# State-space mixer: phases on GpSimd, states of every step summed on TensorE, a skip product of 128 rows

## The chip, the cores and the metric

The kernel runs on one core of one Trainium2 chip. The metric is the device time of one execution in microseconds (us), as a median of runs. In the profile the engines are PE (TensorE; PEld is its weight load), DVE (VectorE), ACT (ScalarE), POOL (GpSimd) and SP (SyncE, which here only issues DMAs).

## The reference

Two layers over 512 tokens of 1024 channels, all in float32. Layer 0 mixes the tokens with a state-space model (S5), layer 1 with causal latent attention; each is followed by a layer norm, a feed-forward part with squared relu, and another norm. The change lies in S5 alone:

```python
# 64 groups of 16 channels, 64 complex states per group
mag = exp(lr * dt);  a = mag * (cos(li * dt) + i sin(li * dt))
bb  = (a - 1) / lam * b
h_t = a * h_(t-1) + bb u_t                    # complex, over 512 tokens
y   = Re(c h) + d_skip * u                    # the skip is d_skip * u
y   = gelu(y)
val, gate = split(y @ w_glu);  mix = (val * sigmoid(gate)) @ w_out
```

## The kernel before

The core runs S5 first (about the first 150 us), then glu, projections, feed-forward and attention, in which TensorE works nearly without a pause. In S5 the 64 groups are cut into eight eighths (e = 0 to 7), one per step of a loop. The 512 tokens are 64 chunks of 8. Real and imaginary parts of 64 states lie on 128 partitions.

Ahead of the loop, `s5_tables` (L157) makes the tables of all groups on VectorE, the phase `f` of a chunk in turns among them, and `s5_powers` (L214) their powers. A step then takes these parts:

- `s5_phase(e)` (L269): r = k f less its nearest integer, for 64 chunks k and 8 groups. It is called twice. The first call makes eight ScalarE products (L275) and one ScalarE addition that rounds (L276); the second is one VectorE operation (L278).
- `s5_trig(e)`: the sine and cosine of r on ScalarE (L284, L287, L288).
- `s5_w`, `s5_q` (L264, L294, L364): outer products W and Q on VectorE.
- `s5_p`: eight transposes of W on TensorE (L304), copied out by ScalarE (L307); `s5_s`: the chunks' inputs (L315).
- `s5_rot`, `s5_add`, `s5_scan` (L323 to L343): rotate by the phase on VectorE, add the swapped half on TensorE (L330, L331), scan over the chunks on VectorE (L341), rotate back.
- `s5_turn` and `s5_state` (L346, L354): the states H = hc + x. In steps 0 and 1 (`S5_WHOLE`) TensorE adds hc too (L351) and ScalarE copies H out of PSUM (L356); in the other six steps TensorE makes x alone (L352) and VectorE adds hc (L359).
- `s5_t`: the response within a chunk, TT, on TensorE with 32 columns of weights (L378, L380), and onto its diagonal the skip d, by products with 32 rows (L384); ScalarE spreads TT (L387). `s5_y`: outputs (L396, L397), then a gelu (L404), a trip through DRAM and a split.

The order on each engine is the order in which the code issues, since S5 runs under a manual schedule. Step e makes the phase of step e + 2. TensorE fills waits with products that nothing reads (`warm`) in steps 0 and 1, and with parts of the glu (L573 to L575) later. Tiles that `self.f` makes come from a ring of ten, so that one may have to wait for the readers of the tile that held its place.

Of the kernel before, what the change touches and what calls it, by code (L numbers as in the profile page):

```python
# [76 lines left out]
class Net:  # L77
# [37 lines left out]
    def turns(self, out, x, tmp):  # L115
        """x less its nearest integer"""
        v = self.nc.vector
        yield v.tensor_scalar(tmp, x, MAGIC, MAGIC, op0=ALU.add, op1=ALU.subtract)
        yield v.tensor_tensor(out, x, tmp, op=ALU.subtract)

    def angle(self, k, out, x):
        """x to [-pi, pi], and its absolute value in k"""
        v = self.nc.vector
        yield v.tensor_scalar(k, x, 1.0 / TWO_PI, MAGIC, op0=ALU.mult, op1=ALU.add)
        yield v.tensor_scalar(k, k, MAGIC, None, op0=ALU.subtract)
        for i, part in enumerate(PI_PARTS):
            yield v.scalar_tensor_tensor(out, k, -part, x if i == 0 else out, op0=ALU.mult, op1=ALU.add)
        yield v.tensor_scalar(out, out, 3.1415925, -3.1415925, op0=ALU.min, op1=ALU.max)
        yield v.scalar_tensor_tensor(k, out, -1.0, out, op0=ALU.mult, op1=ALU.max)
# [27 lines left out]
    def s5_tables(self, pool):  # L157
# [25 lines left out]
        def phase():  # L183
            yield v.tensor_tensor(t1, li, dt, op=ALU.mult)
            yield from self.angle(t2, th, t1)
            nc.scalar.activation(t1, th, AF.Sin)
            nc.scalar.activation(t2, t2, AF.Sin, bias=self.col(3), scale=-1.0)
            # phase of a whole chunk of 8 tokens, in turns
            yield v.tensor_scalar(f, th, 8.0 / TWO_PI, None, op0=ALU.mult)
            yield from self.turns(f, f, t7)  # L190
# [11 lines left out]
        # coef = (a - 1) / lam  # L202
# [11 lines left out]
    def s5_powers(self, pool, i, j):  # L214
        """powers of a, and their products with coef, for eighths i to j"""
# [13 lines left out]
    def s5_static(self, pool):  # L229
        ms = self.nc.gpsimd.memset  # L230
        self.dd = pool.tile([32, 64, 16], F32, name="dd")
        self.nc.sync.dma_start(out=self.dd, in_=self.a["s5d"])
# [25 lines left out]
    def s5_outer(self, pool, e, dst, n, t_re, t_im, i, sign):  # L258
        """three operations, to be issued in turn"""
# [9 lines left out]
    def s5_phase(self, e):  # L269
        """the phase of k chunks, in turns"""  # L270
        st, f = self.st[e], self.tab["f"]
        if "r" not in st:
            st["r"], st["rt"] = self.f("r", [128, 8, 64]), self.f("rt", [128, 8, 64])
            for g in range(8):
                self.nc.scalar.mul(st["r"][:, g, :], self.c[:, C_KK:C_KK + 64], f[:, 8 * e + g:8 * e + g + 1])  # L275
            self.nc.scalar.activation(st["rt"], st["r"], AF.Identity, bias=self.col(8), scale=-1.0)  # L276
        else:
            self.nc.vector.scalar_tensor_tensor(st["r"], st["rt"], MAGIC, st["r"], op0=ALU.subtract, op1=ALU.add)  # L278
# [12 lines left out]
    def s5_w(self, pool, e):  # L291
        """W: response of the state to an input"""
# [5 lines left out]
    def s5_p(self, e):  # L298
        """P = (a W)^T of every group"""
# [10 lines left out]
    def s5_s(self, e):  # L310
        """inputs of the chunks"""
# [7 lines left out]
    # states before every chunk: a real recurrence in the rotating frame  # L319
# [26 lines left out]
    def s5_turn(self, e):  # L346
        self.st[e]["x"] = x = self.psum()
        hc, hs = self.st[e]["g"]
        whole = e in S5_WHOLE
        if whole:  # L350
            self.nc.tensor.matmul(x, self.ident, hc, start=True, stop=False)  # L351
        self.nc.tensor.matmul(x, self.c[:, C_NSW64:C_NSW64 + 128], hs, start=not whole, stop=True)  # L352

    def s5_state(self, e):  # L354
        if e in S5_WHOLE:
            self.nc.scalar.copy(self.H[:, :, 1:64], self.st[e]["x"].rearrange("p (g k) -> p g k", k=64)[:, :, 0:63])  # L356
            return
        hc, x = [z.rearrange("p (g k) -> p g k", k=64)[:, :, 0:63] for z in (self.st[e]["g"][0], self.st[e]["x"])]
        self.nc.vector.tensor_tensor(self.H[:, :, 1:64], hc, x, op=ALU.add)  # L359

    def s5_q(self, pool, e):
        """Q: response to the state before a chunk"""
# [6 lines left out]
    def s5_t(self, e):  # L369
        """TT: response within a chunk, with the skip on its diagonal"""  # L370
        act, pe = self.nc.scalar, self.nc.tensor
        W, TT, Q, one = self.W[e % 2], self.TT[e % 2], self.st[e]["Q"], self.c[0:32, C_E:C_E + 64]
# [16 lines left out]
    def s5_y(self, e):  # L389
        """outputs, in rows (position, channel)"""  # L390
# [9 lines left out]
    def s5_gelu(self, e):  # L400
        """their gelu, in rows (channel, group) by way of DRAM"""
# [12 lines left out]
    def warm(self, out, n, src=None):  # L414
        """products that nothing reads, while there is nothing else: the tensor engine's clock is halved after a pause"""
# [7 lines left out]
    def s5(self, pool, u0, early):  # L423
        """returns the split gelu'd outputs and the sums of the first units of the glu over them, but the last"""
# [13 lines left out]
        self.s5_phase(0)  # L438
# [8 lines left out]
        def partial(n):  # L447
            """some products of the glu that are ready"""
# [10 lines left out]
        for e in range(NT):  # L459
# [5 lines left out]
            if e == 0:  # L465
                self.s5_t(0)
                self.s5_phase(1)
# [35 lines left out]
            if e + 2 < NT:  # L503
                self.s5_phase(e + 2)
# [6 lines left out]
    def weights(self, units):  # L511
        """units: list of (dram AP, shape); loaded and split in this order"""
# [39 lines left out]
    # the second part of a split can be put off, for the vector engine not to wait  # L552
# [24 lines left out]
    def dense_steps(self, ps, w, col, act, tok=slice(0, T), n=None):  # L577
        """ps [128, tokens] = w[:, :, col].T @ act, over the k tiles of act; stops after every one"""
# [20 lines left out]
    def rstd(self, out, sq, n, eps_col):  # L599
        """sq: tiles [128, tokens] of squares, still to be summed over the partitions; n: their number; stops after the sums and before  # L600
        their spreading"""
# [13 lines left out]
        # the mean of s / var and 1 / s, for a root s that is nearly right  # L615
# [17 lines left out]
    class Norm:  # L633
        """z: 8 tiles [128, T] of the channels, normed in place, then split into act or stored to out"""
# [5 lines left out]
        def add(self, j):  # L640
            """z[j] is there"""
# [7 lines left out]
        def mean(self, last=None):  # L649
            """last: a tile that is not in the sum yet"""  # L650
# [10 lines left out]
        def squares(self, parts=(0,)):  # L661
            """z less its mean, and its squares, summed over the tiles from every one of parts to the next"""
# [22 lines left out]
        def finish(self):  # L685
            """stops after every tile"""
# [27 lines left out]
        def keep(self):  # L714
            """the normed z itself, for the next residual; stops after every tile"""
# [5 lines left out]
    def rms_norm(self, x, g, n):  # L721
        """x: tiles in PSUM [128, T]; the split normed tiles, with the tokens put in order; stops after every tile,
        after the sums, before and after their spreading"""
# [26 lines left out]
    # tokens of layer 0 stand in the order (position in a chunk, chunk)  # L750
# [10 lines left out]
    class Ahead:  # L761
        """the first three units of the next layer"""
# [15 lines left out]
    def feed_forward(self, u0, h, act, hid, g, b, follow=None, out=None, aside=iter(())):  # L778
        """hid: the hidden tiles of the first three units; aside: work for the vector engine that fits in"""
# [32 lines left out]
    def boundary(self, u, src, settle, z, g, b, follow=None, out=None, pool=None, begun=None):  # L812
        """the last four units before a layer norm, the norm, and the first three after it: half of the tokens is
        normed while the other is computed"""
# [29 lines left out]
        with self.tc.manual_schedule():  # L844
# [56 lines left out]
            def run2(i, tok, ms=(0, 1)):  # L901
                """both tiles of a unit in turn, for its rows may still be on their way"""
# [42 lines left out]
    def project(self, u0, act, h, g, b, follow, order=None, zpool=None, pool=None, begun=None):  # L945
        """layer norm of ALPHA * h + act @ w, for a [DM, DM] matrix in four units"""
# [32 lines left out]
    def rope(self, x, then):  # L979
        """x [128, T]: two heads of 64 rows; rotated in place"""  # L980
# [78 lines left out]
    def values(self, p, a):  # L1059
        """two of the four token tiles, for both heads"""  # L1060
# [12 lines left out]
    def query_rope(self, p):  # L1073
        """rotary parts of both heads, scaled"""
# [26 lines left out]
    def scores(self, hd, t):  # L1101
        """exponentials of the scores of query tile t [128 queries, keys up to them]"""
# [22 lines left out]
    def transposed(self, hd, t):  # L1125
        """into room for the two parts of p^T of one head: key tile k has the queries from 128 k on"""
# [15 lines left out]
    def attention(self, u0, latent, kvg, qg):  # L1142
# [10 lines left out]
        def fill(steps):  # L1153
            """products of the next layer's first unit with the heads that are there"""
# [11 lines left out]
        def ahead(p, s):  # L1166
            """what the coming queries need, some of it for the next two heads"""
# [50 lines left out]
# eighths whose gelus, and whose splits, are due in a step of S5: gelus in pairs, for fewer loads of tables  # L1218
S5_GELUS = [[0], [1], [], [2, 3], [], [4, 5], [6], [7]]
S5_SPLITS = [[], [0], [1], [], [2], [3], [4], [5, 6]]  # L1220
# steps in which a unit of weights is split; spare products of a step; steps whose states the tensor engine adds up
S5_UNITS = [1, 3, 6]
S5_WARM = [[2, 2, 2], [6, 3, 2]] + 6 * [[0, 0, 0]]
S5_WHOLE = [0, 1]
# [63 lines left out]
def host_s5(x, lam_re, lam_im, log_dt, b_re, b_im, c_re, c_im, d):  # L1288
    """layout only"""
# [16 lines left out]
def layout(x, positions, ln_mix_g, ln_mix_b, ln_ffn_g, ln_ffn_b, w_ff1, w_ff2, ssm_lam_re, ssm_lam_im, ssm_log_dt,  # L1306
# [10 lines left out]
    def cut(w, cols):  # L1317
        """[K, N] -> [units, 128, K / 128, cols]"""
# [40 lines left out]
```

## Time and profile before

| what | us |
|---|---|
| median of 3 runs (1204.53 to 1206.81) | 1206.55 |
| span of the profiled execution, first to last instruction | 1203.0 |
| TensorE busy | 1171.5 (97%) |
| VectorE busy | 693.1 (58%) |
| ScalarE busy | 510.2 (42%) |
| GpSimd busy | 2.6 (0%) |

The profiled execution is listed by its span alone; 3.55 us lie between that and the median. A busy time counts an engine's own instructions, and a matmul's end is modelled, so a full TensorE row says that there was no pause, not that each product was as short as it could be. The shares are of the whole span; S5 has its own, which the rows below give by stretches.

### The profile page before, as it was taken

What the parts mean: (1) busy time and instruction counts of PE and PEld (TensorE: products, weight loads), DVE (VectorE), ACT (ScalarE), POOL (GpSimd) and SP (SyncE); (2) the same over time, 40 slices, a digit from 0 to 9 for tenths busy, and PEclk for the clock granted to TensorE, in tenths of its full rate; (3) what the DMA queues carried; (4) which work ended last, traced back from release to release, by engine and by line L of the source; (5) the groups of instructions that cost most, each with busy time, mean ns of one, the idle gap of its engine ahead of it and who ended that gap; (6) DMA issues with size and microseconds to landing.
All of it is one profiled execution on the core that took longest, in us unless ns stands there. A gap on an engine that the chain in (4) does not pass through costs nothing.

```text
span 1203.0 us, 16076 instructions
## 1 busy us (share of the span) xinstructions
PE 1171.5 (97%) x6634; PEld 1002.4 (83%) x6634; DVE 693.1 (58%) x1244; ACT 510.2 (42%) x867; POOL 2.6 (0%) x12
## 2 busy tenths in 40 slices
PE   5899999999999999999999999999999999999996
PEld 3778888999888888888999788889988888888896
DVE  8999552487444434425585787768733442533456
ACT  4888551337314414213356566534731421322324
POOL 0000000000000000000000000000000000000000
PEclk9999999999999999999999999999999999999998
DMA  4122361214232222323311112221322222331212
GB/s 166 47 89 95 97 205 66 96 45 133 72 120 70 105 105 70 105 105 105 127 35 38 43 51 71 71 72 57 119 70 105 73 103 105 105 105 70 105 36 71
DMA packets 28905, 106.16 MB, mean 88 GB/s; under 512 B 10624, under 2 KB 12800, under 8 KB 18208
## 3 DMA queue, kind: packets, MB, share of 16 engines
q1 hardware_dynamic: 27680, 103.04, 25.1%
q10 hardware_dynamic: 1152, 2.10, 0.5%
q8 instruction: 52, 0.85, 0.3%
q14 instruction: 21, 0.17, 0.0%
HBM read 100.93 MB, written 4.19 MB: 87 GB/s over the span
## 4 chain that ended last, share of the span: by engine, by line
PE 91%; DVE 6%; ACT 2%; issue 1%; DMA 0%; ACTq 0%; DVEq 0%
PE ps L574 27%; PE ps L575 27%; PE ps L573 27%; PE ps L397 1%; PE ps L396 1%; PE ps L315 1%; PE ps L1110 1%; PE ps L380 1%; PE ps L1136 1%; PE ps L607 1%; PE ps L1111 1%; PE ps L352 1%; DVE tmpw L264 1%; PE ps L630 1%; PE ps L330 0%
## 5 line engine op out<-in xcount | busy, mean ns | idle before, releaser
L573 PE MATMUL ps<-hh,whi 128*128 128x512 f32 (+1 forms) x704 | 245.0, 348 | 0.0
L574 PE MATMUL ps<-hl,whi 128*128 128x512 f32 (+1 forms) x704 | 243.7, 346 | 0.0
L575 PE MATMUL ps<-hh,wlo 128*128 128x512 f32 (+1 forms) x704 | 243.6, 346 | 0.0
L530 ACT CAST whi<-raw 128x2048 fp32r<-128x2048 f32 (+1 forms) x91 | 165.9, 1834 | 162.7 <-DMA raw<-in_ff 141.6
L532 DVE TENSOR_TENSOR wlo<-raw,whi 128x1024 fp32r<-128x1024 f32 (+2 forms) x182 | 206.4, 1176 | 30.6 <-ACT whi L530 28.6
L573 PE MATMUL ps<-fh,whi 128*128 128x512 f32 (+1 forms) x608 | 216.8, 357 | 0.0
L574 PE MATMUL ps<-fl,whi 128*128 128x512 f32 (+1 forms) x608 | 216.1, 355 | 0.0
L575 PE MATMUL ps<-fh,wlo 128*128 128x512 f32 (+1 forms) x608 | 216.1, 355 | 0.0
L772 ACT ACTIVATE relu<-ps 128x512 f32<-128x512 f32 x64 | 38.1, 595 | 265.8 <-PE ps L575 265.8
L573 PEld LDWEIGHTS ps<-hh,whi 128*128 128x128 f32 x704 | 133.6, 190 | 16.4
L574 PEld LDWEIGHTS ps<-hl,whi 128*128 128x128 f32 x704 | 133.7, 190 | 16.2
L575 PEld LDWEIGHTS ps<-hh,wlo 128*128 128x128 f32 x704 | 133.7, 190 | 16.1
L774 DVE TENSOR_TENSOR relu<-relu 128x512 f32<-128x512 f32 x64 | 44.2, 690 | 169.2 <-ACT fh L773 169.2
L573 PEld LDWEIGHTS ps<-fh,whi 128*128 128x128 f32 x608 | 114.9, 189 | 16.5
L574 PEld LDWEIGHTS ps<-fl,whi 128*128 128x128 f32 x608 | 114.9, 189 | 16.3
L575 PEld LDWEIGHTS ps<-fh,wlo 128*128 128x128 f32 x608 | 114.9, 189 | 16.1
L790 DVE TENSOR_TENSOR z<-z,ps 128x512 f32<-128x512 f32 (+1 forms) x60 | 34.7, 579 | 119.8 <-PE ps L575 119.8
L573 PE MATMUL ps<-yh,whi 128*128 128x512 f32 x128 | 52.3, 410 | 0.0
L670 ACT ACTIVATE q<-z 128x256 f32<-128x256 f32 x64 | 25.0, 418 | 59.8 <-DVE z L668 59.8
L575 PE MATMUL ps<-yh,wlo 128*128 128x512 f32 x128 | 49.7, 390 | 0.0
L574 PE MATMUL ps<-yl,whi 128*128 128x512 f32 x128 | 49.7, 390 | 0.0
L775 DVE TENSOR_TENSOR fl<-relu,fh 128x512 fp32r<-128x512 f32 x64 | 44.2, 691 | 2.1
(255 smaller groups left out, 1744.3 us busy)
## 6 DMA issues: line engine op xcount, KB each, us to landing
raw<-in_ff SPq DMA_DIRECT2D x64, 1024.0 KB, 4.8
raw<-in_glu SPq DMA_DIRECT2D x8, 1024.0 KB, 5.1
raw<-in_w_out SPq DMA_DIRECT2D x4, 1024.0 KB, 5.0
raw<-in_wo SPq DMA_DIRECT2D x4, 1024.0 KB, 4.7
raw<-in_kvq SPq DMA_DIRECT2D x3, 1024.0 KB, 4.9
raw<-in_attq SPq DMA_DIRECT2D x4, 576.0 KB, 3.8
bc<-in_s5x SPq DMA_DIRECT2D x8, 256.0 KB, 4.6
u<-in_s5x SPq DMA_DIRECT2D x8, 256.0 KB, 5.1
```

Source lines behind the costliest of these rows:

```text
L264: v.tensor_tensor(o, self.tab[t][:, 0:n, G].rearrange("p m g -> p g m").unsqueeze(3).to_broadcast([128, 8, n, 16]), bc[:, j].unsqueeze(2). ...
L315: self.nc.tensor.matmul(s[:, g * 64:g * 64 + 64], st["P"][g // 4][:, 128 * (g % 4):128 * (g % 4) + 128], st["U"][:, g, :], start=True, sto ...
L530: self.nc.scalar.copy(hi, raw)
L532: self.put_off(lambda c=c: self.nc.vector.tensor_tensor(lo[:, c], raw[:, c], hi[:, c].bitcast(F32), op=ALU.subtract))
L573: pe.matmul(ps, whi, ahi, start=start, stop=False)
L574: pe.matmul(ps, whi, alo, start=False, stop=False)
L575: pe.matmul(ps, wlo, ahi, start=False, stop=stop)
L670: act.activation(qs[j], zj, AF.Square)
L772: self.nc.scalar.activation(r, ps, AF.Relu)
L774: self.nc.vector.tensor_tensor(r, r, r, op=ALU.mult)
L775: self.nc.vector.tensor_tensor(lo, r, hi.bitcast(F32), op=ALU.subtract)
L790: v.tensor_tensor(z[m][:, tok], z[m][:, tok], ps, op=ALU.add)
```

## The change

It has three parts, and comments and docstrings are gone throughout.

```diff
-        self.dd = pool.tile([32, 64, 16], F32, name="dd")
-        self.nc.sync.dma_start(out=self.dd, in_=self.a["s5d"])
+        self.dd = pool.tile([128, 64, 16], F32, name="dd")
+        for rows in (slice(32, 64), slice(64, 128)):
+            ms(self.dd[rows], 0.0)
+        self.nc.sync.dma_start(out=self.dd[0:32], in_=self.a["s5d"])
...
     def s5_phase(self, e):
-        st, f = self.st[e], self.tab["f"]
-        if "r" not in st:
-            st["r"], st["rt"] = self.f("r", [128, 8, 64]), self.f("rt", [128, 8, 64])
-            for g in range(8):
-                self.nc.scalar.mul(st["r"][:, g, :], self.c[:, C_KK:C_KK + 64], f[:, 8 * e + g:8 * e + g + 1])
-            self.nc.scalar.activation(st["rt"], st["r"], AF.Identity, bias=self.col(8), scale=-1.0)
-        else:
-            self.nc.vector.scalar_tensor_tensor(st["r"], st["rt"], MAGIC, st["r"], op0=ALU.subtract, op1=ALU.add)
+        st, p = self.st[e], self.nc.gpsimd
+        r, rt = st["r"], st["rt"] = self.f("r", [128, 8, 64]), self.f("rt", [128, 8, 64])
+        p.tensor_tensor(r, self.c[:, C_KK:C_KK + 64].unsqueeze(1).to_broadcast([128, 8, 64]),
+                        self.tab["f"][:, 8 * e:8 * e + 8].unsqueeze(2).to_broadcast([128, 8, 64]), op=ALU.mult)
+        p.tensor_scalar(rt, r, MAGIC, MAGIC, op0=ALU.add, op1=ALU.subtract)
+        p.tensor_tensor(r, r, rt, op=ALU.subtract)
...
     def s5_turn(self, e):
-        whole = e in S5_WHOLE
-        if whole:
-            self.nc.tensor.matmul(x, self.ident, hc, start=True, stop=False)
-        self.nc.tensor.matmul(x, self.c[:, C_NSW64:C_NSW64 + 128], hs, start=not whole, stop=True)
+        self.nc.tensor.matmul(x, self.ident, hc, start=True, stop=False)
+        self.nc.tensor.matmul(x, self.c[:, C_NSW64:C_NSW64 + 128], hs, start=False, stop=True)
...
     def s5_state(self, e):
-        if e in S5_WHOLE:
-            self.nc.scalar.copy(self.H[:, :, 1:64], self.st[e]["x"].rearrange("p (g k) -> p g k", k=64)[:, :, 0:63])
-            return
-        hc, x = [z.rearrange("p (g k) -> p g k", k=64)[:, :, 0:63] for z in (self.st[e]["g"][0], self.st[e]["x"])]
-        self.nc.vector.tensor_tensor(self.H[:, :, 1:64], hc, x, op=ALU.add)
+        self.nc.scalar.copy(self.H[:, :, 1:64], self.st[e]["x"].rearrange("p (g k) -> p g k", k=64)[:, :, 0:63])
...
-        W, TT, Q, one = self.W[e % 2], self.TT[e % 2], self.st[e]["Q"], self.c[0:32, C_E:C_E + 64]
+        W, TT, Q, one = self.W[e % 2], self.TT[e % 2], self.st[e]["Q"], self.c[:, C_E:C_E + 64]
```

The second calls of `s5_phase` are gone from `s5`, and so is `S5_WHOLE`. The 96 added rows of `dd` are zero.

On GpSimd (POOL) the program had, behind the memsets of the tables, nothing up to its end:

```order
L240 MEMSET H 128x8
L242 MEMSET TT_186 128x1024
L242 MEMSET TT_187 128x1024
L1354 UNCONDITIONAL_BRANCH
L1354 ISA [waits barrier_Pool_Activation_PE_DVE_SP_gather]
```

It now has, in the same place, three operations for each of the eight phases, of which the first three phases are (r_203 is the phase of step 0, r_240 of step 1, r_381 of step 2):

```order
L244 MEMSET TT_189 128x1024
L275 ISA
L275 TENSOR_TENSOR r_203<-c,f 128x512 [waits DMAHW1_49,DVE_49]
L277 TENSOR_SCALAR rt_204<-r_203 128x512 [waits Pool_49]
L278 TENSOR_TENSOR r_203<-r_203,rt_204 128x512 [waits Pool_49]
L275 TENSOR_TENSOR r_240<-c,f 128x512
L277 TENSOR_SCALAR rt_241<-r_240 128x512 [waits Pool_49]
L278 TENSOR_TENSOR r_240<-r_240,rt_241 128x512 [waits Pool_49]
L275 TENSOR_TENSOR r_381<-c,f 128x512 [waits Activation_49]
L277 TENSOR_SCALAR rt_382<-r_381 128x512 [waits Activation_49,Pool_49]
L278 TENSOR_TENSOR r_381<-r_381,rt_382 128x512 [waits Pool_49]
```

The first waits for the table `f` from VectorE; nothing holds the next six but what is named, so GpSimd takes them one behind the other.

On ScalarE (ACT), at the same place, before (behind the two sines of the tables):

```order
L275 ACTIVATE r_201<-c,f 128x64 [waits DVE_49]
L275 ACTIVATE r_201<-c,f 128x64 x7
L276 ACTIVATE rt_202<-r_201,c 128x512 [waits Activation_49]
L275 ACTIVATE r_244<-c,f 128x64 x8
L276 ACTIVATE rt_245<-r_244,c 128x512 [waits Activation_49]
L284 ACTIVATE rt_202<-r_201 128x512 [waits DVE_49]
L307 COPY P_268<-ps_263 128x512 [waits PE_49]
```

and now:

```order
L284 ACTIVATE rt_204<-r_203 128x512 [waits Pool_49]
L307 COPY P_257<-ps_252 128x512 [waits PE_49]
L307 COPY P_264<-ps_259 128x512 [waits PE_49]
L287 ACTIVATE si_250<-r_203,c 128x512
L288 ACTIVATE co_249<-rt_204,c 128x512 [waits Activation_49]
```

The products of the phase are out of this queue; L284 waits for GpSimd now, with the copies of P behind it. On VectorE the L278 rows are gone and the rows around them keep their order.

On TensorE (PE), in step 2 (ps_676 is x, ps_684 the inputs of step 3), before:

```order
L304 MATMUL ps_655<-c,W_190 128x128 x4
L304 MATMUL ps_662<-c,W_190 128x128 x4
L352 MATMUL ps_676<-hs_671,c 128x512
L315 MATMUL ps_684<-u_297,P_660 128x64 x4
L315 MATMUL ps_684<-u_297,P_667 128x64 x4
```

and now (ps_650 is x):

```order
L304 MATMUL ps_629<-c,W_192 128x128 x4
L304 MATMUL ps_636<-c,W_192 128x128 x4
L349 MATMUL ps_650<-hc_644,c 128x512
L350 MATMUL ps_650<-hs_645,c 128x512
L315 MATMUL ps_659<-u_286,P_634 128x64 x4
L315 MATMUL ps_659<-u_286,P_641 128x64 x4
```

One product more stands between the transposes and the inputs of the next step; the same holds in steps 3 to 7.

## Rows read from the trace of the kernel before

**Rows 1.** Engines by stretch (start:end, length, busy us, clock, DMA share, GB/s).
```profile
20.00:40.00 20.00, 18.18 (x135) 14.07 (x136) 19.86 (x37) 14.35 (x31) 0.00 (x0) 1.00 0.00 1
...
60.00:80.00 20.00, 19.45 (x149) 14.95 (x150) 18.87 (x20) 16.40 (x37) 0.00 (x0) 1.00 0.35 118
80.00:100.00 20.00, 19.53 (x151) 15.97 (x149) 19.63 (x22) 18.95 (x41) 0.00 (x0) 1.00 0.47 132
100.00:120.00 20.00, 20.00 (x174) 16.70 (x174) 18.45 (x21) 14.71 (x33) 0.00 (x0) 1.00 0.08 28
```
**Rows 2.** Chain that ended last, 0 to 280 us (start, length, engine, tile, line).
```profile
20.16 0.60 DVE r L278
...
24.26 0.68 DVE gc L323
...
31.99 0.60 DVE hs L343
...
48.57 0.64 PE ps L304 x4
...
105.00 1.06 PE ps L330 x2
...
110.56 0.86 PE ps L352 x2
...
119.67 1.06 PE ps L330 x2
```
**Rows 3.** Timeline, VectorE and GpSimd, 0 to 10 us (start, length; idle in brackets).
```profile
1.25 1.84 POOL L242 MEMSET TT<- 128x1024 f32 x2
...
2.80 0.34 DVE L133 TENSOR_SCALAR scr<-par 128x64 f32<-128x64 f32 x1 [2.80 <-DMA par<-in_s5p]
...
6.91 0.19 DVE L133 TENSOR_SCALAR scr<-scr 128x64 f32<-128x64 f32 x1
...
9.29 0.22 DVE L119 TENSOR_TENSOR f<-f,scr 128x64 f32<-128x64 f32 x1
```
**Rows 4.** GpSimd memsets by line (ns minimum/median/maximum).
```profile
L238 POOL MEMSET W<- x2: 205/206/207, 0.9 to 1.0; 128x128 f32 x2
...
L242 POOL MEMSET TT<- x2: 953/953/953, 1.3 to 2.1; 128x1024 f32 x2
```
**Rows 5.** Timeline, ScalarE, 14 to 50 us.
```profile
20.79 0.63 ACT L284 ACTIVATE rt<-r 128x512 f32<-128x512 f32 x1 [5.82 <-DVE r L278]
...
22.27 0.73 ACT L287 ACTIVATE si<-r,c 128x512 f32<-128x512 f32 x1
...
47.39 0.72 ACT L287 ACTIVATE si<-r,c 128x512 f32<-128x512 f32 x1
```
**Rows 6.** Timeline, TensorE, step 4: the skip's products and their neighbours.
```profile
117.44 0.21 PE L378 MATMUL ps<-Q,W 128*32 128x16 f32 x2
117.50 0.36 PE L380 MATMUL ps<-Q,W 128*32 128x112 f32 x2
117.79 0.41 PE L384 MATMUL ps<-dd,c 32*32 32x64 f32 x4
118.13 0.23 PE L378 MATMUL ps<-Q,W 128*32 128x16 f32 x2
118.21 0.36 PE L380 MATMUL ps<-Q,W 128*32 128x112 f32 x2
118.41 0.21 PE L378 MATMUL ps<-Q,W 128*32 128x16 f32 x2
```
**Rows 7.** Waits, 16 to 150 us (waiter, releaser, us in total, times, longest).
```profile
PEld ps L384 <- issue: 2.8, 16, 0.2
```
**Rows 8.** Timeline, TensorE, steps 2 and 3: pauses in brackets.
```profile
66.51 1.10 PE L352 MATMUL ps<-hs,c 128*128 128x512 f32 x2 [0.55 <-ACT si L287]
...
80.75 1.10 PE L352 MATMUL ps<-hs,c 128*128 128x512 f32 x2 [0.47 <-DVE hs L343]
```
**Rows 9.** ScalarE products that go, by line (ns minimum/median/maximum).
```profile
L275 ACT ACTIVATE r<-c,f x64: 331/337/363, 9.5 to 113.8; 128x64 f32<-128x64 f32 x64
```

More of the change, by code (lines that the diff above doesn't have):

```diff
@@ L437, in s5 @@
         self.s5_w(pool, 0)
-        self.s5_phase(0)
         self.s5_trig(0, self.s5_p)
@@ L466, in s5 @@
                 self.s5_t(0)
-                self.s5_phase(1)
             partial(2 * early)
@@ L502, in s5 @@
                 self.s5_powers(pool, 2, NT)
-            if e + 2 < NT:
-                self.s5_phase(e + 2)
         partial(len(todo))
@@ L1223 @@
 S5_WARM = [[2, 2, 2], [6, 3, 2]] + 6 * [[0, 0, 0]]
-S5_WHOLE = [0, 1]
 FILL = {26: 4, 29: 2, 30: 4, 31: 1, 33: 1, 35: 2}
```

## Prediction

> **What bounds the kernel now.** I read the busy times by stretch first, since 97% for TensorE is an average: from 20 to 40 us VectorE is busy 19.86 of 20 us and TensorE 18.18, and from 100 us TensorE is full while VectorE has room [rows 1]. Then the chain that ended last: it runs through VectorE from the tables on, with three L278 operations of 0.60 us each in it (the first stands in the rows), and passes to TensorE at 48.57 with the transposes of step 2 [rows 2]. Then the TensorE timeline from there on: it is back to back but for two pauses, 0.55 us in step 2 and 0.47 us in step 3, both in front of L352 [rows 8]. So S5 has two stretches. Up to 48 us a VectorE operation costs its time. Behind it TensorE's work costs its time, and work on VectorE or ScalarE costs nothing as long as it has room. VectorE's room is small: 0.37 us in the 20 us from 80 to 100, 1.13 us from 60 to 80, 1.55 us from 100 to 120 [rows 1].
>
> **The change part by part.** The profiled execution is given by its span of 1203.0 us, 3.55 us under the median; I work out a difference and add it to the median of 1206.55.
>
> *(a) L278 leaves VectorE.* Of eight, three are in the VectorE stretch's chain [rows 2]: 3 x 0.60 = -1.8 us. What would be late next there: gc of step 0 waits for the products L315, and these for the copies of P, which stand behind an L284 that waited 5.82 us for L278 [rows 5]. With r ready early, L284 is done long before and the copies follow the transposes directly, so they move forward by about as much. The other five L278 lie in TensorE's stretch and give nothing but room.
>
> *(b) Seven GpSimd operations come as one burst.* `f` is there at about 9.5 us [rows 3]; the phases of steps 0 and 1 and the first product of step 2 then run one after the other. No row shows such an operation. The nearest are memsets: 206 ns for 128 columns and 953 ns for 1024 [rows 4], that is 0.83 ns a column, or 0.53 us for 512. A memset moves one stream; a tensor_scalar reads one and writes one; a tensor_tensor reads two and writes one. If streams overlap where they can, they take 0.53 and 1.05 us; if none do, 1.05 and 1.58. I take 1.05 for a tensor_tensor and 0.53 for a tensor_scalar, the ends nearer to the rows, thus 2.6 us for a phase.
>
> Do they hide? On GpSimd itself, yes: r of step 0 is wanted at 20.79 [rows 5], and three operations from 9.5 us end near 12. The question is VectorE, which in these microseconds issues short operations with two operands in the same memory, all of them in the chain. The trace has one place where both engines work: L133 at 2.80 us ran beside a memset that ended at 3.09, took 0.34 us, and ended at 3.14; the same form took 0.19 later, with GpSimd idle [rows 3]. So it ended just behind the memset and lost 0.15 us. It was VectorE's first instruction, which might account for that as well; but I read it as VectorE having to wait while GpSimd holds the memory's port. Bounds for an operation of GpSimd in this stretch: nothing, if the row is a cold start, and its whole time, if VectorE stands still for it. I take the whole time: 5 x 1.05 + 2 x 0.53 = +6.3 us.
>
> The Trainium skill says so outright (SBUF: State Buffer, "Who interferes with whom"): a VectorE instruction with two SBUF inputs, or in a two-port mode, and a GpSimd instruction that reads SBUF exclude each other for a whole instruction. The row of L133 agrees in direction, with a memset. The page GPSIMD Engine Reference ("Performance versus the Vector engine") gives 4497 ns for a tensor_tensor of 2048 columns; a quarter is an estimate of 1.12 us, by which the burst would be 0.4 us longer.
>
> *(c) Three later places in the VectorE stretch.* The rest of step 2's phase waits until the sine of step 0 has freed its place, 22.27 + 0.73 us [rows 5]; about then VectorE turns to gc and gs, which read one operand from PSUM, so of its 1.58 us (0.53 + 1.05) I charge 0.5. The first product of step 3 takes the place of hs of step 0, made at 31.99 [rows 2], so it falls among the outer products: 1.05. Its rest waits for the sine of step 2, at 47.39 + 0.72 [rows 5], where TensorE takes over: 0.8 of 1.58. Together +2.35 us; at the upper prices about 3.8.
>
> *(d) TensorE in steps 2 to 7.* L351 comes in six steps. Such a product, in its two instructions, takes 0.86 us in the chain [rows 2]: +5.2. It needs hc alone, which VectorE makes ahead of hs, so it fills the two pauses of 0.55 and 0.47 [rows 8]: -1.0. The skip's products: a regular L380 is followed 0.20 us later by the next L378 (118.21 to 118.41), but with L384 between them it takes from 117.50 to 118.13, 0.63 us [rows 6]. So the block costs 0.43 us, and each time its weight load stood still for 0.17 us (2.8 us for 16) [rows 7]. With 128 rows the products have the form of their neighbours (128*32). A neighbour's two instructions take 0.06 us at 16 columns (117.44 to 117.50) and 0.20 at 112, hence 0.13 at 64, and four 0.26. Saved: about 0.18 us, twice a step, in six steps: -2.2. Bounds: nothing, if the block costs the same, and 0.31 a block (-3.8), if columns don't count and four take 2 x 0.06. Sum of (d): 5.2 - 1.0 - 2.2 = +2.0, from +0.4 to +4.2.
>
> The Trainium skill (TensorE: Matmul & The Clock Gate, "Why this matters for your kernels") says that a product of 32 rows takes as long as one of 128. By that the saving would be nil and (d) +4.2; the rows show a stop in front of the 32-row block, which the rule leaves out, and I go by the rows.
>
> *(e) VectorE's room in step 3.* GpSimd takes 2.6 us of VectorE's time a step; L278 and L359 give back 1.2 (an L278 takes 0.60 in the chain [rows 2], and L359 has as many elements). In steps 2 and 4 the room of 0.8 and 1.1 us per step of 14.67 (from 105.00 to 119.67) [rows 1, 2], with 0.5 that TensorE's own growth gives, covers the rest. In step 3 it is 0.27, so some 1.0 us is missing: +1.0, and up to 2 at the upper prices.
>
> *Free.* ScalarE loses 64 x 0.337 = 21.6 us of products [rows 9] and eight L276, and gets six copies of H; it is off the chain in TensorE's stretch. A copy of H stands behind the two copies of P and that of D, in front of yh, and TensorE wants it behind L315. By its place that is close: what it comes later than L315's end shows in L397, some tenths of a us at most. The two memsets of `dd` (953 ns each by [rows 4]) end ahead of the burst. The added wait of L284 on GpSimd has the copies of P behind it, for which L315 waits; it costs nothing while r is there by 20.8 us. SP's and GpSimd's queues pass no DMA.
>
> Sum: -1.8 + 6.3 + 2.35 + 2.0 + 1.0 = +9.85 us, **1216.4 us**.
>
> **The rivals.**
>
> *A: GpSimd does not disturb VectorE.* Then (b), (c) and (e) are nothing and -1.8 + 2.0 = +0.2 remains: 1206.75, between 1205.2 and 1209.0 with the ends of (d). For it: L133's delay may be a first instruction's. Against it: it ended exactly behind the memset. This is the one on the other side: not slower. It decides if a VectorE operation beside a GpSimd one keeps its length.
>
> *B: faster.* As A, with the skip's block at its low end (+0.4 for (d)), and the relief of ScalarE bringing the copies of P in steps 2 and 3 forward by as much again as the pauses, 1.0: -2.4, 1204.15. For it: the pause of 0.55 names ScalarE [rows 8]. Against: TensorE's work grows in every case, and there is no other pause to close.
>
> *C: GpSimd is late.* If an operation takes more than (20.8 - 9.5) / 3 = 3.8 us, L284 and behind it the copies of P are late. At 5 us each, without disturbing VectorE, r of step 0 comes at 24.5, 3.7 late, and later phases have steps to spare: 0.2 + 3.7 = +3.9, 1210.45. It includes the new ISA row ahead of the first product, of which the trace shows nothing. For it: broadcast operands and an unknown start. Against: memsets at 0.83 ns a column.
>
> **How the numbers follow.** Forecast 0.55, A 0.28, B 0.10, C 0.07. What a measurement of this kernel can tell from no change is 0.2%, 2.4 us. The forecast and C are slower; A is the same for 0.23 of its 0.28, faster for 0.03 and slower for 0.02; B is faster for 0.09 and the same for 0.01. So faster 0.12, same 0.24, slower 0.64. The likeliest's own range: with 2.35 us less if the later places hide, and 6 us more by the upper prices (burst 10.0, later 3.8, (e) 2), 1211 to 1222. The whole range takes in A, B and C: 1204 to 1222. A granted clock under the 1.00 that these stretches show [rows 1], if TensorE's pauses grow in the burst, would lie at the upper end.
>
> **What would show it.** (a) no L278 on VectorE; (b) from 9.5 to about 20 us VectorE operations of 64 to 144 columns that take over 1 us instead of 0.2 to 0.3, each ending with a GpSimd operation, and the first gc some 5 us later than 24.26 [rows 2] rather than 0.6 earlier; (d) the skip's products without the 0.17 us stop ahead of them, the next product some 0.45 us behind the last one with 112 columns instead of 0.63, and steps 4 to 6 about 0.5 us longer than 14.67; (e) pauses of TensorE in step 3. The forecast is wrong if VectorE's short operations keep their length beside GpSimd's.

## The result, and the profile after

The changed kernel takes 1214.22 us in the median of 4 runs (1213.26 to 1216.01); the kernel before took 1206.61 (1204.53 to 1206.81) beside it. The ratio is 1.0076, with a 95% interval of 1.0058 to 1.0094. By the ratio it is slower by 9.2 us (7.0 to 11.3), where 9.85 were forecast; the two medians alone differ by 7.6. The spans of the two profiled executions, 1211.5 and 1203.0, differ by 8.5 us, but that is not what S5 lost. Here is one product that stands behind S5, and the stretch from 652 to 664 us, each before and then after:

```profile
227.87 0.28 PE L573 MATMUL ps<-gh,whi 128*128 128x256 f32 x1
237.32 0.28 PE L563 MATMUL ps<-gh,whi 128*128 128x256 f32 x1
...
652.00:664.00 12.00, 10.75 (x73) 10.35 (x73) 7.68 (x20) 7.21 (x12) 0.00 (x0) 0.84 0.11 42
652.00:664.00 12.00, 10.98 (x92) 10.81 (x92) 4.49 (x12) 7.44 (x11) 0.00 (x0) 1.00 0.16 51
```

Behind S5 the changed kernel is 9.45 us late. Between 651 and 670 us it makes up 1.4 of them (from the first to the second group of TensorE's two-column products there it is 9.17 us, and 10.56 before). The change touches nothing there; TensorE's granted clock (the column behind GpSimd's) was 0.84 in this stretch of the profile before, and 1.00 in the one after.

Engines of the changed kernel by stretch, in the columns of [rows 1]:

```profile
20.00:40.00 20.00, 16.91 (x88) 11.73 (x87) 17.82 (x23) 5.53 (x12) 4.34 (x3) 0.74 0.00 0
...
60.00:80.00 20.00, 19.75 (x161) 17.07 (x159) 19.59 (x18) 13.24 (x22) 9.29 (x5) 1.00 0.41 132
...
100.00:120.00 20.00, 20.00 (x140) 15.94 (x139) 19.86 (x17) 12.41 (x23) 11.02 (x6) 1.00 0.19 52
```

Against [rows 1] two things are new in the first row: VectorE is busy 17.82 us instead of 19.86, so it waited, and TensorE's granted clock is 0.74 instead of 1.00 (0.57 from 24 to 36 us, near the lower of its two levels, 1.2 and 2.4 GHz). From 60 us on VectorE's room has nearly gone.

VectorE and GpSimd, 0 to 22 us, a timeline (start, length, engine, line, operation):

```profile
1.03 1.93 POOL L233 MEMSET dd<- 32x1024 f32 x2
...
3.31 1.12 DVE L135 TENSOR_SCALAR scr<-scr 128x64 f32<-128x64 f32 x1
...
3.44 1.88 POOL L244 MEMSET TT<- 128x1024 f32 x2
...
10.38 1.06 POOL L275 TENSOR_TENSOR r<-c,f 128x512 f32<-128x512 f32 x1 [5.06 <-DVE f L119]
...
11.52 1.92 POOL L277 TENSOR_SCALAR rt<-r 128x512 f32<-128x512 f32 x1
11.55 0.66 DVE L140 SCALAR_TENSOR_TENSOR scr<-scr,scr 128x64 f32<-128x64 f32 x1
...
13.53 1.27 POOL L278 TENSOR_TENSOR r<-r,rt 128x512 f32<-128x512 f32 x1
13.55 1.32 DVE L204 TENSOR_TENSOR scr<-pi,par 128x64 f32<-128x64 f32 x1
...
17.89 1.33 POOL L278 TENSOR_TENSOR r<-r,rt 128x512 f32<-128x512 f32 x1
...
18.01 1.26 DVE L153 TENSOR_TENSOR pr<-pr,tmp 128x32 f32<-128x32 f32 x1
...
21.28 0.30 DVE L154 TENSOR_TENSOR wi<-wi,tmp 128x144 f32<-128x144 f32 x1
```

Pair each long VectorE row with the GpSimd row above or below it: L204 ends at 14.87, L278 at 14.80; L153 ends at 19.27, L278 at 19.22. An operation of 32 or 64 columns that takes 0.2 us elsewhere lasts as long as GpSimd's two-operand one. Beside the L277 of 1.92 us VectorE lost only 0.44 (L140, 0.66 for 0.22). At 3.31 the same happens to an L135 (1.12 for 0.19) under the memsets of TT, which the new memsets of `dd` had pushed there. In the kernel below that has these memsets and nothing else new on GpSimd, the tables end 0.8 us late (last L154 at 16.67 instead of 15.87). Here the last L154 of the tables begins at 21.28, 5.4 us later than before.

TensorE and VectorE, 25 to 54 us:

```profile
25.63 1.97 PE L304 MATMUL ps<-c,W 128*128 128x128 f32 x8 [2.23 <-DVE W L294]
...
27.42 3.68 PE L315 MATMUL ps<-u,P 128*128 128x64 f32 x16
...
31.21 0.69 DVE L323 TENSOR_TENSOR gc<-co,ps 128x512 f32<-128x512 f32 x1 [2.04 <-PE ps L315]
...
32.41 2.23 DVE L266 TENSOR_TENSOR W<-wr,bc 128x1152 f32<-128x1152 f32 x1
...
53.64 1.65 DVE L294 SCALAR_TENSOR_TENSOR W<-tmpw,c,W 128x1152 f32<-128x1152 f32 x1
```

TensorE stood still for 2.23 us until W came, then did its products at half clock: L315 took 3.68 us, and 2.00 in the kernel with a longer fill below, which kept 1.00. So VectorE had to wait 2.04 us for the chunks' inputs (L315), and the first gc came at 31.21 instead of 24.26 [rows 2]. The L266 and the L294 take 0.88 and 0.23 us over their usual 1.35 and 1.42, beside GpSimd's next phases.

TensorE, steps 3 to 6: a pause, the skip block of step 4, and the heads of steps 5 and 6:

```profile
87.74 1.10 PE L349 MATMUL ps<-hc,c 128*128 128x512 f32 x2 [0.79 <-DVE hc L342]
...
110.96 0.36 PE L374 MATMUL ps<-Q,W 128*32 128x112 f32 x2
...
111.16 0.39 PE L378 MATMUL ps<-dd,c 128*32 128x64 f32 x4
...
111.38 0.21 PE L372 MATMUL ps<-Q,W 128*32 128x16 f32 x2
...
112.72 1.13 PE L330 MATMUL ps<-gc,c 128*128 128x512 f32 x2
...
127.89 1.12 PE L330 MATMUL ps<-gc,c 128*128 128x512 f32 x2
```

A step takes 15.17 us where it took 14.67 [rows 2]. From the last 112-column product to the one behind the skip it is 0.42 us instead of 0.63 [rows 6] (those rows are of step 5, if the heads are counted as here).

### The profile page after: what moved, and what is told of

Its sections match the earlier page's. It is cut to its first block, busy times and chain, and to the rows that moved or that the text cites. A ratio compares the mean times of both kernels' runs of the same rounds, so it can differ in the third digit from the quotient of the medians.

```text
span 1211.5 us, 16061 instructions
## 1 busy us (share of the span) xinstructions
PE 1177.2 (97%) x6646; PEld 1007.7 (83%) x6646; DVE 699.2 (58%) x1230; ACT 492.3 (41%) x801; POOL 46.0 (4%) x38
## 3 DMA queue, kind: packets, MB, share of 16 engines
q10 hardware_dynamic: 1152, 2.10, 0.5%
## 4 chain that ended last, share of the span: by engine, by line
PE 90%; DVE 7%; ACT 2%; issue 1%; DMA 0%; ACTq 0%; DVEq 0%
PE ps L565 27%; PE ps L564 27%; PE ps L563 27%; PE ps L315 1%; PE ps L1100 1%; PE ps L391 1%; PE ps L390 1%; DVE tmpw L266 1%; PE ps L597 1%; PE ps L1126 1%; PE ps L374 1%; PE ps L1101 1%; PE ps L330 0%; PE ps L349 0%; PE ps L620 0%
```

## The experiments

The theory was the prediction's: GpSimd's operations stop VectorE's short ones and delay the first steps, and TensorE's later steps grow by 0.50 us each. The main rival: GpSimd does not disturb, and what is lost comes from the added products, from waits on GpSimd's results, or from TensorE's clock. Ratios are to the kernel before, run beside each; 0.001 is 1.2 us. The diffs are cut to the lines that matter; names in angle brackets stand for longer expressions.

### The three parts, each by itself

GpSimd alone (the kernel before with the phases on GpSimd):

```diff
+        p.tensor_tensor(r, <kk>, <f>, op=ALU.mult)
+        p.tensor_scalar(rt, r, MAGIC, MAGIC, op0=ALU.add, op1=ALU.subtract)
+        p.tensor_tensor(r, r, rt, op=ALU.subtract)
...
```

> The kernel before with the phases on GpSimd, nothing else. Theory (VectorE stands still while GpSimd reads two operands, and TensorE's clock falls in the pause that this makes): the first gc comes about 6 us later than 24.26, granted clock under 1.00 in 20 to 40 us, total +5 to +6.5 us, 1211.6 to 1213.1. Rival (GpSimd does not disturb, the loss is TensorE's added products): -1.8 us, 1204.8, clock 1.00.

Measured: 1211.66 us, ratio 1.0057 (1.0044 to 1.0070), or +6.9 us, with 5.3 to 8.4 in the interval: the highest of the three parts, though the interval overlaps with the next one's.

The sums alone (the kernel before with the states of all steps summed on TensorE):

```diff
-        self.nc.tensor.matmul(x, self.c[:, C_NSW64:C_NSW64 + 128], hs, start=not whole, stop=True)
+        self.nc.tensor.matmul(x, self.ident, hc, start=True, stop=False)
+        self.nc.tensor.matmul(x, self.c[:, C_NSW64:C_NSW64 + 128], hs, start=False, stop=True)
...
```

> The kernel before with the states of all steps summed on TensorE, nothing else. Theory (TensorE bounds steps 2 to 7, two pauses of 0.55 and 0.47 us are filled): 6 x 0.86 - 1.0 = +4.2 us, 1210.8; steps 4 to 6 take 15.53 us instead of 14.67. Rival (VectorE's relief of six L359 gives it back): 0 to +1 us.

Measured: 1210.76 us, ratio 1.0049 (1.0037 to 1.0062), +5.9 us (4.5 to 7.5). Heads of steps 6 and 7 in its timeline:

```profile
123.81 1.12 PE L330 MATMUL ps<-gc,c 128*128 128x512 f32 x2
...
139.31 1.12 PE L330 MATMUL ps<-gc,c 128*128 128x512 f32 x2
```

The step between them takes 15.50 us, 0.83 more than before: the 0.86 of the added product, nearly whole. The price per step is confirmed. The whole is above the 4.2 us of the forecast's terms (5.2 - 1.0): the profiled execution had lost 1.7 us by the head of step 2, where its clock fell between 48 and 56 us (0.79). The profile of the skip alone, next, shows 0.79 there as well, without these products, so the fall is not shown to come from them.

The skip alone (the kernel before with 128 rows, and with the two memsets of `dd`):

```diff
+        for rows in (slice(32, 64), slice(64, 128)):
+            ms(self.dd[rows], 0.0)
...
-        W, TT, Q, one = self.W[e % 2], self.TT[e % 2], self.st[e]["Q"], self.c[0:32, C_E:C_E + 64]
+        W, TT, Q, one = self.W[e % 2], self.TT[e % 2], self.st[e]["Q"], self.c[:, C_E:C_E + 64]
```

> The kernel before with the skip's products of 128 rows, nothing else. Theory (a block saves 0.21 us, twice a step, in steps 2 to 7; the two added memsets cost 0.8 us on VectorE's first operations): -2.5 + 0.8 = -1.7 us, 1204.9. Rival (a product of 32 rows takes as long as one of 128): only the memsets remain, +0.8 us.

Measured: 1202.92 us, ratio 0.9984 (0.9974 to 0.9994), -1.9 us (-3.1 to -0.7). The part that adds rows makes the kernel faster.

Both TensorE parts, without GpSimd (the changed kernel with the phases made as before):

```diff
-        p.tensor_tensor(r, <kk>, <f>, op=ALU.mult)
+                self.nc.scalar.mul(st["r"][:, g, :], <kk>, f[:, 8 * e + g:8 * e + g + 1])
```

> The changed kernel with the phases back on ScalarE and VectorE. Theory (the phases are the loss, the two other parts +2.5 us together): 1209.1, against 1214.2 with the phases on GpSimd. Rival (the loss is TensorE's added products): it stays at 1213 or above.

Measured: 1208.83 us, ratio 1.0031 (1.0020 to 1.0042): the sum of the two (0.0049 - 0.0016). So what is left for GpSimd in the changed kernel is 0.0045, about 5.4 us. The traces say the same: behind S5 this kernel is 3.9 us later than the kernel before, and the changed one 9.45, which leaves 5.6.

### Does GpSimd disturb VectorE, or is its result late?

The kernel before, with the same six GpSimd operations of the first two phases put in behind `f`. They write into a W that is not yet in use, nobody reads what they made, and the phases come from ScalarE and VectorE as ever:

```diff
+        for e in range(2):
+            p.tensor_tensor(sr, <kk>, <f of e>, op=ALU.mult)
+            p.tensor_scalar(srt, sr, MAGIC, MAGIC, op0=ALU.add, op1=ALU.subtract)
+            p.tensor_tensor(sr, sr, srt, op=ALU.subtract)
```

> The kernel before, in which GpSimd also works through the six operations of the first two phases, at the same place, into a part of W[1] that is overwritten later; nothing reads them, and the phases stay on ScalarE and VectorE. Theory (the loss is VectorE standing still beside GpSimd): tables late by about 4.6 us (last L154 of the tables at 20.5 instead of 15.87), granted clock under 1.00 in 24 to 36 us, total +5 to +7 us. Rival (the loss comes from waiting for GpSimd's results): no change.

Measured: 1210.76 us, ratio 1.0048 (1.0029 to 1.0066). VectorE and GpSimd in its timeline:

```profile
12.73 1.27 POOL L438 TENSOR_TENSOR W<-W 128x512 f32<-128x512 f32 x1
12.76 1.33 DVE L204 TENSOR_TENSOR scr<-pi,par 128x64 f32<-128x64 f32 x1
...
17.22 1.30 POOL L438 TENSOR_TENSOR W<-W 128x512 f32<-128x512 f32 x1
...
17.32 1.25 DVE L154 TENSOR_TENSOR pi<-pi,tmp 128x32 f32<-128x32 f32 x1
...
30.32 0.69 DVE L323 TENSOR_TENSOR gc<-co,ps 128x512 f32<-128x512 f32 x1 [1.39 <-PE ps L315]
```

The same stops, and gc 6.06 us late, with no wait on GpSimd anywhere; the tables end 4.6 us late (last L154 at 20.45). This refutes rival A: the engines collide, and no dependence is needed.

Is it any work of GpSimd, or that which reads? Nine memsets in the same place, 9.02 us in all:

```diff
+        p.tensor_copy(self.W[1][:, 0, 1, 0:1], self.tab["f"][:, 0:1])
+        for _ in range(9):
+            p.memset(self.W[1][:, :, 1:9, :], 0.0)
```

> The kernel before, in which GpSimd writes nine memsets of 1024 columns (0.95 us each, 8.6 us in all) into that part of W[1] from the moment that f is there. Theory (a VectorE operation with two operands loses its second read to a GpSimd that reads, and only tensor_scalar and casts are stopped by one that writes): three VectorE operations of the tables lose up to 0.95 us each, +1 to +3 us. Rival (any GpSimd operation stops VectorE): tables late by about 8 us, +8 us or more.

Measured: 1205.41 us, ratio 1.0008 (0.9993 to 1.0022), no change that can be told.

```profile
9.84 9.02 POOL L435 MEMSET W<- 128x1024 f32 x9
...
9.91 0.93 DVE L146 CAST scr<-scr 128x64 int32<-128x64 f32 x1
...
12.09 0.77 DVE L203 TENSOR_SCALAR scr<-pr 128x64 f32<-128x64 f32 x1
...
13.71 0.17 DVE L152 TENSOR_TENSOR pr<-pr 128x16 f32<-128x16 f32 x1
...
16.88 0.30 DVE L154 TENSOR_TENSOR wi<-wi,tmp 128x144 f32<-128x144 f32 x1
```

Beside memsets VectorE's two-operand operations keep their length (L152, 0.17 us), and only a cast and a tensor_scalar are stopped; the tables end 1.0 us late instead of 4.6. So what counts is which kinds meet. The Trainium skill (SBUF: State Buffer, "Who interferes with whom") has just this: a VectorE operation with two SBUF inputs collides with a GpSimd one that reads SBUF and not with one that only writes, while casts and tensor_scalars can collide by way of their two-port modes. Both runs agree with it, but for one form: GpSimd's tensor_scalar reads SBUF too, and in the burst each of 1.92 us stopped a two-operand operation of VectorE for 0.44 only.

### Does the fallen clock cost the end anything?

The changed kernel with more fill products ahead of the first transposes, 9 and 4 instead of 5 and 2:

```diff
-        self.warm(acc[-1], 5, <dec>)
+        self.warm(acc[-1], 9, <dec>)
-        self.warm(acc[-1], 2, <wr>)
+        self.warm(acc[-1], 4, <wr>)
```

> The changed kernel with nine instead of five fill products on dec and four instead of two on wr, so that TensorE does not pause while VectorE is held up. Theory (2.1 us of the loss are products at half the clock between 24 and 36 us, for which the first gc waited): granted clock 1.00 there, the first gc about 2 us earlier than 31.21, total 2 us under the changed kernel, ratio 1.0058 to the kernel before. Rival (VectorE alone sets that time): no change, ratio 1.0076.

Measured: 1214.54 us, ratio 1.0082 (1.0064 to 1.0101), against 1.0076: nothing gained. Its windows, and lines of TensorE's and VectorE's timelines:

```profile
20.00:40.00 20.00, 18.59 (x102) 11.27 (x101) 19.40 (x24) 8.98 (x19) 5.75 (x3) 1.00 0.00 1
52.00:64.00 12.00, 9.46 (x40) 6.56 (x39) 9.91 (x10) 7.21 (x10) 2.51 (x2) 0.72 0.06 22
```

```profile
27.48 2.00 PE L315 MATMUL ps<-u,P 128*128 128x64 f32 x16 [0.24 <-ACT P L307]
...
29.59 0.69 DVE L323 TENSOR_TENSOR gc<-co,ps 128x512 f32<-128x512 f32 x1 [0.46 <-PE ps L315]
...
54.83 1.94 PE L304 MATMUL ps<-c,W 128*128 128x128 f32 x8 [2.54 <-DVE W L294]
```

The clock held in the first stretch and the first gc came at 29.59, 1.6 us earlier than 31.21. Then a pause of 2.54 us opened ahead of the transposes of step 2, and the clock fell there. So I filled that pause too, with ten more products in step 1 (the first stretch keeps its longer fill):

```diff
-S5_WARM = [[2, 2, 2], [6, 3, 2]] + 6 * [[0, 0, 0]]
+S5_WARM = [[2, 2, 2], [16, 3, 2]] + 6 * [[0, 0, 0]]
```

> The changed kernel with 9 and 4 fill products instead of 5 and 2 ahead of the first transposes, and 16 instead of 6 in step 1. Theory: with the longer fill at the start the granted clock stays at 1.00 in 24 to 36 us, and ten more fill products of 0.2 us close most of TensorE's pause of 2.54 us ahead of the transposes of step 2 (L304 at 54.83), so that the clock stays at 1.00 in 52 to 64 us as well: 2 to 3 us under the changed kernel, ratio 1.005 to 1.006, some 1211.5 us. Rival: what the clock cost is taken by the next wait (VectorE's W, ScalarE), and the time stays at 1.0076 to 1.0082.

Measured: 1214.55 us, ratio 1.0087 (1.0073 to 1.0101). The granted clock is 1.00 in every stretch from 20 to 70 us, and the time is the same; the expectation failed. VectorE in its timeline:

```profile
30.57 0.69 DVE L323 TENSOR_TENSOR gc<-co,ps 128x512 f32<-128x512 f32 x1 [1.43 <-PE ps L315]
...
33.05 2.42 DVE L266 TENSOR_TENSOR tmpw<-wi,bc 128x1152 f32<-128x1152 f32 x1
...
50.55 1.70 DVE L266 TENSOR_TENSOR W<-wr,bc 128x1152 f32<-128x1152 f32 x1
...
53.55 2.34 DVE L294 SCALAR_TENSOR_TENSOR W<-tmpw,c,W 128x1152 f32<-128x1152 f32 x1
```

The fill held the transposes up until 27.19 instead of 25.63, so gc won 0.64 us only. (In the kernel with the first fill alone they began at 26.21. The first stretch is the same code in both: there the same eighteen products of the fill took 9.65 us, here 10.62.) And GpSimd's phases of steps 2 and 3 now met more of VectorE's outer products: 1.07 + 0.35 + 0.92 = 2.34 us over their usual lengths, against 0.88 + 0.23 in the changed kernel. Part of step 2's phase had run there while VectorE waited (29.16 to 31.21). The fallen clock is visible, but that it costs the end is not shown: each time it was kept up, another stop took its place.

### How much is the burst, how much the later phases?

The changed kernel with the phases of steps 0 and 1 made as before and only those of steps 2 to 7 on GpSimd:

```diff
+            if e < 2:
+                <eight products and the addition on ScalarE>
+                return
             p.tensor_tensor(r, <kk>, <f>, op=ALU.mult)
```

> The changed kernel, but the phases of chunks 0 and 1 made as before (ScalarE and VectorE); those of chunks 2 to 7 stay on GpSimd. Theory: the loss of the GpSimd part is the burst beside the tables and the clock that falls behind it; with the burst gone the tables end near 16.7 us (15.87 before, and 0.8 for the two memsets of dd), the granted clock in 24 to 36 us is 1.00, the first gc starts near 25 us, and the time is that of the kernel with the two other parts alone (ratio 1.0031) or a little over it for the phases of step 3 and later: ratio 1.003 to 1.004, some 1209 us. Rival: the phases of the later steps cost as much as the first two, by the lengths of VectorE's operations beside them (L266 2.2 us against 1.35): ratio 1.006 or over.

Measured: 1210.76 us, ratio 1.0052 (1.0040 to 1.0065). It lies between theory (1.003 to 1.004) and rival (1.006). So the burst costs the changed kernel 0.0024, some 2.9 us, and the later phases 0.0021 over the kernel without GpSimd, some 2.5 us. Each is a difference of two ratios, and uncertain by some 2 us. VectorE and GpSimd in its timeline:

```profile
23.86 2.15 DVE L366 SCALAR_TENSOR_TENSOR Q<-Q,c,tmpw 128x1024 f32<-128x1024 f32 x1
...
27.87 2.32 POOL L284 TENSOR_TENSOR r<-r,rt 128x512 f32<-128x512 f32 x1
...
29.00 2.42 DVE L266 TENSOR_TENSOR tmpw<-wi,bc 128x1152 f32<-128x1152 f32 x1
...
46.49 1.69 DVE L266 TENSOR_TENSOR W<-wr,bc 128x1152 f32<-128x1152 f32 x1
...
49.48 2.30 DVE L302 SCALAR_TENSOR_TENSOR W<-tmpw,c,W 128x1152 f32<-128x1152 f32 x1
...
51.71 1.21 DVE L349 TENSOR_TENSOR_SCAN ga<-D,ps 128x512 f32<-128x512 f32 x1
```

Over the usual lengths (1.28, 1.35, 1.35, 1.42) these four lose 0.87 + 1.07 + 0.34 + 0.88 = 3.16 us; one L278 less gives back 0.60; the second scan comes 2.55 us later than in the kernel without GpSimd (51.71 against 49.16). Up to that scan the sum closes.

### Versions that might be faster

The kernel before, with GpSimd's late phases and the 128-row skip, its zero rows brought by the DMA (the host's layout has them):

```diff
-        self.dd = pool.tile([32, 64, 16], F32, name="dd")
+        self.dd = pool.tile([128, 64, 16], F32, name="dd")
...
+        <phases 2 to 7 on GpSimd, as above>
...
-    dd = np.zeros((32, 64, 16), np.float32)
+    dd = np.zeros((128, 64, 16), np.float32)
```

> The kernel before with the phases of chunks 2 to 7 alone on GpSimd, and the skip's product with 128 rows whose zero rows come with the DMA. Theory: TensorE sets the pace of steps 4 to 7, GpSimd's work there is beside it, and the skip blocks give back 0.18 to 0.21 us each; without a burst nothing is lost in steps 0 and 1: 1 to 2.5 us under the kernel before (ratio 0.998 to 0.999). Rival: VectorE's longer operations beside GpSimd delay steps 2 to 4 by as much as the skip blocks save: ratio 0.9995 or over.

Measured: 1207.43 us, ratio 1.0025 (1.0015 to 1.0036); the rival held. The late phases undo the skip's gain.

The same skip without GpSimd, and five more fill products in step 1 against the clock's fall near 50 us:

```diff
-        self.dd = pool.tile([32, 64, 16], F32, name="dd")
+        self.dd = pool.tile([128, 64, 16], F32, name="dd")
...
-S5_WARM = [[2, 2, 2], [6, 3, 2]] + 6 * [[0, 0, 0]]
+S5_WARM = [[2, 2, 2], [11, 3, 2]] + 6 * [[0, 0, 0]]
```

> The kernel before with the skip's products of 128 rows alone, the zero rows coming with the load instead of memsets, and 11 instead of 6 fill products in step 1 ahead of the transposes of step 2 (1.15 us in the pause of 1.30). Theory: -2.5 us for the products, and another -1 us because the clock no longer falls at 50 us in some executions; 1201.5, faster than both kernels. Rival (the longer load or the fill products cost as much): 1203 or above.

Measured: 1203.49 us, ratio 0.9989 (0.9980 to 0.9999). Its TensorE timeline in step 2:

```profile
66.51 1.10 PE L352 MATMUL ps<-hs,c 128*128 128x512 f32 x2 [0.89 <-ACT si L287]
```

The pause was 0.55 us [rows 8], and this product starts at 66.51 in both kernels: what the skip blocks of step 1 saved comes back here as a wait for ScalarE. Some of the later savings are lost in waits too; behind S5 1.25 us are left (the product with gh at 226.62 instead of 227.87). It is faster than both kernels by a little, and no better than the skip's part alone (0.9984); the fill is not shown to help.

## Why the prediction was nearly right

By its steps, against the two profiled executions. At the head of step 2 the changed kernel is 6.67 us behind (61.72 before, 68.39 after), and behind S5 9.45; the later 1.4 us of the clock have nothing to do with the sum.

```profile
61.72 1.12 PE L330 MATMUL ps<-gc,c 128*128 128x512 f32 x2
68.39 1.12 PE L330 MATMUL ps<-gc,c 128*128 128x512 f32 x2
```

- **(a)** -1.8 us: as forecast. No L278 is left on VectorE (in the changed kernel L278 is a line of GpSimd).
- **(b)** The mechanism was right: stops of VectorE in the burst, each about as long as GpSimd's two-operand operation beside it. The size was off, 6.3 forecast and 4.6 found. There were six operations, not seven, since step 2's first product waited for a sine of step 0, as the order shown with the change already said. The two-operand ones took 1.04 to 1.33 us, near the 1.05 assumed. The tensor_scalar took 1.92 us instead of 0.53, but stopped VectorE for some 0.45 only: my rule of whole times was wrong for it, and the two errors nearly cancelled. And the row that I read it from was luck: L133 beside a memset is a tensor_scalar, and memsets do stop those, but they leave two-operand operations alone, and it was these that the burst stopped.
- **Free work.** The memsets of `dd` were put at nothing since they end ahead of the burst. They pushed the memsets of TT onto an L135, +0.8 us. I had looked at when they end, not at what they delay in GpSimd's own queue. The rest was free: no pause of TensorE from step 2 on ends with a copy of H, and L284 had r at 14.80, long before the 20.8 of rival C.
- **Not in the sum:** the wait of 2.04 us at the first gc, with the fallen clock. The prediction named the clock as something for the upper end. It counts in this execution; that the end would be earlier without it is not shown (above).
- **(c)** 2.35 forecast, 0.88 + 0.23 = 1.1 found, since part of step 2's phase fell into VectorE's wait. Without that wait the same phases stop VectorE for 3.16 us (late phases alone).
- So up to step 2: -1.8 + 4.6 + 0.8 + 2.0 + 1.1 = 6.7, against 6.67 found. That it closes so well is partly chance: the skip blocks of step 1, which save some 0.35 us, are not in it, nor is an hc of 0.84 us instead of 0.69, nor what the rounding takes.
- **(d)** Near the forecast: steps 5 and 6 grow by 0.50 us each (0.86, less twice 0.18; the block saves 0.21), step 4 by 0.29, and step 2 by nothing, its pause filled. The 0.83 that a step grows by the product alone bears out the first term. The saving is tested less closely: the -1.9 us of the skip alone have a wide interval and the memsets in them, and the last kernel above keeps 1.25 behind S5, where 2.2 were forecast.
- **(e)** Step 3 grew by 0.86 us. (d) gives 0.50 of that and the filled pause takes 0.47 away, so 0.83 are left for (e), against 1.0; the pause of 0.79 for hc stands in the profile after. From the head of step 2 to the end of S5 the changed kernel loses 2.78 us (9.45 - 6.67), where (d) and (e) together had 3.0.

Rival A fell by the run whose GpSimd results nobody reads, B by the sign, C by the time of r. That 9.85 came so near rests partly on errors that cancel: a burst that was 1.7 too dear, later places 1.2 too dear, and 2.8 us of memsets and waiting that were left out. The ratio's interval is 4 us wide, so the sum is not tested closer than that. The lower end of the likeliest's range, 1211, does not follow from its own sentence: 2.35 us less than 1216.4 are 1214.05.

## What to carry to other kernels

Before moving work to an engine that is idle, ask which operations of the busy one will run beside it, and of what kinds: the same six operations cost 5.8 us with nobody reading their results, and nine memsets in their place nothing that could be measured. Split a change into its parts: here the one that seemed to add work (rows of zeros) gained 1.9 us, and the two others lost. A wait that appears in a trace is not yet a cost: fill it, and see whether the end moves.

## What the runs showed that was not expected

GpSimd's tensor_scalar, with one tensor operand and two constants, takes longer than its tensor_tensor: 1.92 us against 1.04 to 1.33 for 512 columns. The Trainium skill (GPSIMD Engine Reference, "Performance versus the Vector engine") has 4497 ns for a tensor_tensor of 2048 columns; the estimate of 1.12 us made from it lies within these rows. In later steps, beside VectorE's outer products of 1024 and 1152 columns, both stretch: L277 up to 3.39 us, L275 up to 2.02.
